# Attention scores of a head pair in one visit of TensorE, with the eighth result in the first bank, and fillers aligned to it

## The chip, the cores and the metric

One Trainium2 chip; the kernel runs on one of its cores. The metric is the device time of one execution in microseconds (us), as the median of several runs. PE is the matrix engine, DVE the vector engine, ACT the scalar engine, POOL the general one, SP the engine that issues most transfers.

## The reference, cut to what matters

One layer of an encoder on a (512, 1024) residual stream. An input projection feeds two groups that run beside each other: gated linear recurrences (forward and backward), and eight attention heads of 64 with relative bias over dilated windows. Their outputs go through `w_out`, then an MLP with squared ReLU, then a final norm.

```python
h = rms_norm(x, attn_norm_g)
xr, gate, q, k, v = split(h @ w_in)
xr = centred_depthwise_conv(xr, conv_w, conv_b)
y_rnn = (rg_lru(xr, fwd) + rg_lru(xr, bwd)) * gelu(gate)
# dilated_attention: 8 heads, patterns (window, dilation) = (128,1), (512,4), (2048,16)
logits = einsum('bqhd,bqjhd->bhqj', qb, k[:, kidx]) * 64 ** -0.5 + bias   # masked outside 0..511
out_p, lse_p = softmax(logits) @ v[:, kidx], logsumexp(logits)            # for each pattern
y_attn = sum_p softmax_p(lse_p) * out_p
x = x + concat(rms_norm(y_rnn, g1), rms_norm(y_attn, g2)) @ w_out
x = x + square(relu(rms_norm(x, g3) @ w_up)) @ w_down
return rms_norm(x, final_norm_g)
```

## The kernel before, in words

**Arithmetic.** A float32 product is made of three matmuls: both factors are split into a high part and a remainder, and `mm3` adds high x high, high x low and low x high in one PSUM bank. `conv_hi` makes the high part of a weight chunk (ACT, tile `whi`), `conv_lo` the remainder (DVE, `wlo`) and then issues the load of a later chunk (`wraw`, an SP transfer of 512 KB).

**Attention.** Positions are ordered by parity, and all three patterns are one banded score matrix with a bias table, so a query tile of 128 meets 416 keys (`NK`). The heads go in four pairs `p`; head e of a pair lies on rows 64e to 64e+63. The four query tiles of a pair have the numbers u = 0 to 3 in order of their work. `att_s` (L796 to L803 before) is the scores: for each u, three products, each for both heads, into two PSUM banks; the two heads' matmuls use 64 rows each of the array. `kks[p]` holds the keys of a pair, high and low, and behind the first 512 columns a copy of the first 256, which an SP transfer makes in `s_lo`; tiles u = 2 and 3 read into that copy. `att_e` subtracts the minimum and adds the bias on DVE (one operation for each head, PSUM to `e`) and takes the exponential on ACT. `att_t` turns three blocks of the result on PE (`pt`, banks `et`), ACT copies them to `ett`, and `att_c` turns the last 32 columns on DVE. `att_z` and `att_zd` send the reciprocal sums through DRAM and back as rows (`zd`, `zrow`), `att_av` multiplies with the values (`pav`). `load_tw` loads the bias rows of two heads (`tw`, 192 and 160 KB).

**PSUM.** Eight banks under three tags: `gs` has two, `et` two, `pj` four. A bank is taken again when its last reader is done.

**Order.** The order of every engine is that of the program text. The loop at the end of the attention part runs over i = 0 to 4 and u = 0 to 3: in round i, pair i gets its scores while pair i-1 gets its transposes. Around these stand *fillers*: one filler is one k of eight of a query or key projection (`q_thunks`, three matmuls, 0.68 us), later one of four of an output projection (`wo_thunks`). `PRE` fillers run ahead of the loop, then four in each (i, u) unless `FILL` says otherwise. `feed_q` places a weight split at two fillers of a chunk. `plan` hangs small steps (`beside`) on places (i, u, 0 to 4): among them `s_hi` and `s_lo`, which split the queries (is_k 0) and keys (is_k 1) of the next pair. SP's transfers in the loop are issued in program order too, so one that waits holds up those behind it.

Before the change a pair's scores come in two groups, u = 0 and 1, and u = 2 and 3, with eight fillers between, and a group's 12 matmuls go product by product over both tiles.

Of the kernel before, what the change touches and what calls it, by code (L numbers as in the profile page):

```python
# [28 lines left out]
NEG = -1e30  # L29
DFF = 4096  # L30
NF = DFF // P
PRE = 6
SC = (20, 21, 22, 23, 24, 25, 26, 27, 40, 41, 43, 45, 47, 49, 51, 53)
HF = NF // 2
NQ = HF // 4
# [2 lines left out]
WN = 160  # L38
# [60 lines left out]
def hybrid_kernel(ctx: ExitStack, tc, xw0, xw, xn, w_in, w_v, w_out, w_up, w_dn, gates, vecs, bias, fg, out):  # L99
# [19 lines left out]
    def ps_(name, tag):  # L119
        return psum.tile([P, S], FT, name=name, tag=tag, bufs={"pj": 4, "gs": 2, "et": 2}[tag])  # L120
# [182 lines left out]
            conv_lo(c + 3)  # L303

    def feed_q(c, k):
        if k == 1:
            conv_hi(c + 3)
        elif k == 5:
            conv_lo(c + 3)

    def mm3(o, a, b, first, last, on=False):
        nc.tensor.matmul(o, lhsT=a[0], rhs=b[0], start=bool(first), stop=False, skip_group_check=on)  # L312
# [479 lines left out]
    QT = ((1, 0), (1, 1), (0, 0), (0, 1))  # L792
    QSEQ = (0, 3, 1, 2)

    def att_s(p, us):
        for u in us:  # L796
            psq[p, u] = [ps_("ps", "pj" if u % 2 else "gs") for _ in range(2)]
        for i, (a, b) in enumerate(((0, 0), (0, 1), (1, 0))):
            for u in us:
                qt = QSEQ[u]  # L800
                w = {(0, 0): TH + TH - WN, (0, 1): 0, (1, 0): TH - WN, (1, 1): TH}[QT[qt]]
                for e, r in enumerate(halves):
                    nc.tensor.matmul(psq[p, u][e][:, :NK], lhsT=qs_[p, a][r, P * qt:P * qt + P], rhs=kks[p][r, b, w:w + NK], start=i == 0, stop=i == 2)  # L803

    def att_e(p, u):
        qt = QSEQ[u]
# [171 lines left out]
    def wo_thunks():  # L978
        order = [(0, tt, k) for tt in range(4) for k in range(4)] + [(1, tt, k) for h in (0, 2) for tt in range(4) for k in (h, h + 1)]
        pw = {}  # L980

        def end(n, tt):
            stt(x1[tt, n], pw[n, tt], rc[0][:, tt:tt + 1], x1[tt, n], op0=OP.mult, op1=OP.add)

        def mk(b, n, tt, k):
            def run():
                if k == 0:
                    pw[n, tt] = ps_("pwo", "pj")
                o = pw[n, tt]
                hi, lo = splits[C_WO + 2 * n + k // 2]  # L990
                sl, tsl = slice((k % 2) * S, (k % 2 + 1) * S), slice(tt * P, (tt + 1) * P)
                mm3(o, [t[:, tsl] for t in ycat[k]], (hi[:, sl], lo[:, sl]), k == 0, k == 3)
                if b in (1, 15, 18, 23):
                    conv_hi(C_WO + {1: 3, 15: 4, 18: 5, 23: 6}[b])
                if b in (3, 17, 20):
                    conv_lo(C_WO + {3: 3, 17: 4, 20: 5}[b])
                if n == 0 and tt and k == 1:
                    end(0, tt - 1)
                if n and (tt, k) == (0, 1):
                    end(0, 3)  # L1000
                if n and k == 3 and tt < 3:
                    end(1, tt)
            return run
        st["wo"] = lambda: end(1, 3)
        return [mk(b, *o) for b, o in enumerate(order)]
# [88 lines left out]
    def sq_(t):  # L1094
        return lambda: rnn_sq(t)
# [4 lines left out]
    def op(fn, *a):  # L1100
# [5 lines left out]
            (0, 2, 3): [add],  # L1106
            (1, 0, 2): [end(2)],
            (1, 1, 0): [sq_(2)], (1, 1, 2): [end(3)], (1, 1, 4): [add],
            (1, 3, 0): [sq_(3)], (1, 3, 2): [hi(0)], (1, 3, 3): [add, hi(1)], (2, 0, 2): [rnn_cols],
            (2, 0, 0): [lo(0), lo(1)], (2, 0, 4): [hi(2)],  # L1110
            (2, 1, 2): [hi(3)], (2, 1, 4): [lo(2)], (2, 2, 3): [lo(3)]}
    for i in range(3):
        for key, (is_k, fn) in {(0, 2): (0, s_hi), (1, 0): (0, s_lo), (2, 2): (1, s_hi), (3, 0): (1, s_lo)}.items():
            plan.setdefault((i,) + key, []).append(lambda fn=fn, a=(i + 1, is_k): fn(*a))

    def beside(*key):
# [10 lines left out]
    for key, fs in (((4, 1, 2), [(att_a, 2), (o_sum, "s1", 0), (o_sum, "s2", 0), (o_sum, "s3", 0), (o_sum, "s3", 1), (o_sum, "22", 0)]),  # L1127
# [1 line left out]
                    ((4, 3, 0), [(att_q, 2), (o_hi, "11", 1), (o_hi, "s3", 0), (o_hi, "s3", 1)]), ((4, 3, 2), [(o_lo, "11", 1), (o_lo, "s3", 0)]),  # L1129
                    ((4, 3, 4), [(att_y, 2), (o_lo, "s3", 1), (o_hi2, 0), (o_hi, "s1", 0), (o_hi, "22", 0)])):  # L1130
        plan[key] = [op(*a) for a in fs]
    FILL = {(3, 0): (1, 1, 1, 0), (3, 1): (1, 1, 1, 0), (3, 2): (1, 1, 1, 0), (4, 0): (0, 1, 0, 0), (4, 1): (0, 1, 0, 1), (4, 2): (0, 1, 0, 0), (4, 3): (0, 1, 0, 0)}


    AVS = {(2, 1): (0,), (4, 0): (1, 2)}
    with tc.manual_schedule(engines={nc.sync.engine}):
        for i in range(5):
            for u in range(4):
                if i < 4:
                    if u % 2 == 0:  # L1140
                        att_s(i, (u, u + 1))
                    if u == 2 and i < 3 or u == 0 and i:
                        for e in range(2):
                            load_tw(2 * (i + u // 2) + e, u // 2)
                if i >= 1:
                    att_t(2 * i - 2, u)
                    att_t(2 * i - 1, u)
                if i < 4:
                    att_e(i, u)
                if i >= 1:  # L1150
                    att_c(2 * i - 2, u)
                    att_c(2 * i - 1, u)
                if u == 0 and i >= 1:
                    att_z(i - 1)
                for p in AVS.get((i, u), ()):
# [7 lines left out]
                for p in AVS.get((i, u), ()):  # L1163
                    if p != 2:
                        att_y(p)
                beside(i, u, 2)
                fill(FILL.get((i, u), (1, 1, 1, 1))[2])
                beside(i, u, 3)
                fill(FILL.get((i, u), (1, 1, 1, 1))[3])
                add_x()  # L1170
                beside(i, u, 4)
    assert not plan and not more
# [631 lines left out]
```

## Time and profile before

| what | us |
|---|---|
| median of 3 runs | 526.63 (526.25 to 527.54) |
| the profiled execution | 526.41 |
| its span, first to last instruction | 524.6 |
| granted clock of TensorE | 0.999 |
| PE busy | 517.5 |
| scores (`ps`, 96 matmuls) between | 93.6 and 152.0 |

The profile's rows give a start or a count, the engine, the line, the operation and the tile written, then the tiles read. Matmuls are pipelined: one 128x512 matmul shows 0.39 us, but the next starts 0.23 us after it, so what a stretch of PE costs is read from starts, not from durations. The same holds for DVE.

### The profile page before, as it was taken

What the parts mean: (1) busy time and instruction counts of PE and PEld (TensorE: products, weight loads), DVE (VectorE), ACT (ScalarE), POOL (GpSimd) and SP (SyncE); (2) the same over time, 40 slices, a digit from 0 to 9 for tenths busy, and PEclk for the clock granted to TensorE, in tenths of its full rate; (3) what the DMA queues carried; (4) which work ended last, traced back from release to release, by engine and by line L of the source; (5) the groups of instructions that cost most, each with busy time, mean ns of one, the idle gap of its engine ahead of it and who ended that gap; (6) DMA issues with size and microseconds to landing.
All of it is one profiled execution on the core that took longest, in us unless ns stands there. A gap on an engine that the chain in (4) does not pass through costs nothing.

```text
span 524.6 us, 8198 instructions
## 1 busy us (share of the span) xinstructions
PE 517.5 (99%) x3021; PEld 443.1 (84%) x3021; DVE 430.5 (82%) x669; ACT 350.4 (67%) x566; POOL 64.0 (12%) x88
## 2 busy tenths in 40 slices
PE   9999999999999999999999999999999999999995
PEld 7867888787787688899999888889999999888884
DVE  6998986888877998898789986889656988885985
ACT  7579946668865748585578666565477677655664
POOL 0182000000000221001300312001101300140000
PEclk9999999999999999999999999999999999999999
DMA  8745545357695299847595899976978497799804
GB/s 288 237 117 166 151 152 180 107 166 208 193 292 192 78 186 279 323 128 196 136 226 144 212 272 281 314 261 161 295 224 205 111 226 219 155 285 256 196 1 161
DMA packets 39961, 104.62 MB, mean 199 GB/s; under 512 B 4944, under 2 KB 13264, under 8 KB 39920
## 3 DMA queue, kind: packets, MB, share of 16 engines
q1 hardware_dynamic: 32368, 78.10, 44.3%
q0 software_dynamic: 7408, 25.79, 26.7%
q8 instruction: 24, 0.39, 0.3%
q10 hardware_dynamic: 144, 0.20, 0.1%
q14 instruction: 17, 0.14, 0.1%
HBM read 95.59 MB, written 4.29 MB: 190 GB/s over the span
## 4 chain that ended last, share of the span: by engine, by line
PE 97%; DVE 2%; issue 0%; DVEq 0%; ACT 0%; ACTq 0%
PE pu L314 10%; PE pu L313 10%; PE pu L312 10%; PE pd L313 10%; PE pd L314 10%; PE pd L312 10%; PE pqk L312 3%; PE pqk L314 3%; PE pqk L313 3%; PE pwo L312 2%; PE pav L939 2%; PE pwo L314 2%; PE pwo L313 2%; PE pt L839 2%; PE ps L803 2%; PE pp L312 1%
## 5 line engine op out<-in xcount | busy, mean ns | idle before, releaser
L269 DVE TENSOR_TENSOR wlo<-wraw,whi 128x1024 fp32r<-128x1024 f32 x71 | 86.7, 1222 | 23.3 <-ACT whi L247 23.1
L247 ACT ACTIVATE whi<-wraw 128x1024 fp32r<-128x1024 f32 x67 | 70.7, 1057 | 33.1 <-PE pd L314 18.2
L313 PE MATMUL pd<-wlo,ah 128*128 128x512 f32 (+1 forms) x195 | 75.3, 386 | 0.0
L312 PE MATMUL pd<-whi,ah 128*128 128x512 f32 (+1 forms) x195 | 75.2, 386 | 0.0
L314 PE MATMUL pd<-whi,al 128*128 128x512 f32 (+1 forms) x195 | 75.2, 386 | 0.0
L247 ACT ACTIVATE whi<-tw 128x1024 fp32r<-128x1024 f32 x38 | 40.2, 1059 | 37.5 <-DMA tw<-in_w_up_dram 12.3
L314 PE MATMUL pu<-hh,wlo 128*128 128x256 f32 x224 | 63.4, 283 | 0.0
L313 PE MATMUL pu<-hl,whi 128*128 128x256 f32 x224 | 63.4, 283 | 0.0
L312 PE MATMUL pu<-hh,whi 128*128 128x256 f32 x224 | 63.4, 283 | 0.0
L269 DVE TENSOR_TENSOR wlo<-tw,whi 128x1024 fp32r<-128x1024 f32 x38 | 46.4, 1222 | 17.8 <-ACT whi L247 17.8
L312 PE MATMUL pu<-h2h,whi 128*128 128x256 f32 (+1 forms) x200 | 60.1, 301 | 0.0
L314 PE MATMUL pu<-h2h,wlo 128*128 128x256 f32 (+1 forms) x200 | 60.0, 300 | 0.0
L313 PE MATMUL pu<-h2l,whi 128*128 128x256 f32 (+1 forms) x200 | 60.0, 300 | 0.0
L247 ACT ACTIVATE whi<-ts 128x1024 fp32r<-128x1024 f32 x24 | 25.5, 1061 | 26.6 <-PE pd L314 17.8
L313 PEld LDWEIGHTS pu<-hl,whi 128*128 128x128 f32 x224 | 43.0, 192 | 0.0
L312 PEld LDWEIGHTS pu<-hh,whi 128*128 128x128 f32 x224 | 43.0, 192 | 0.0
L314 PEld LDWEIGHTS pu<-hh,wlo 128*128 128x128 f32 x224 | 43.0, 192 | 0.0
L312 PEld LDWEIGHTS pd<-whi,ah 128*128 128x128 f32 x195 | 36.6, 188 | 7.5
L314 PEld LDWEIGHTS pd<-whi,al 128*128 128x128 f32 x195 | 36.6, 188 | 7.3
L313 PEld LDWEIGHTS pd<-wlo,ah 128*128 128x128 f32 x195 | 36.6, 188 | 7.3
L269 DVE TENSOR_TENSOR wlo<-ts,whi 128x1024 fp32r<-128x1024 f32 x24 | 29.3, 1222 | 12.5 <-ACT whi L247 12.4
L312 PEld LDWEIGHTS pu<-h2h,whi 128*128 128x128 f32 x200 | 38.3, 191 | 1.3
(275 smaller groups left out, 1225.3 us busy)
## 6 DMA issues: line engine op xcount, KB each, us to landing
wraw<-in_w_up_dram SPq DMA_DIRECT2D x25, 512.0 KB, 4.8
ts<-in_w_dn_dram POOLq DMA_DIRECT2D x24, 512.0 KB, 12.6
wraw<-in_w_dn_dram SPq DMA_DIRECT2D x24, 512.0 KB, 8.7
tw<-in_w_up_dram SPq DMA_DIRECT2D x15, 512.0 KB, 9.2
tw<-in_w_up_dram POOLq DMA_DIRECT2D x15, 512.0 KB, 8.3
wraw<-in_w_in_dram SPq DMA_DIRECT2D x13, 512.0 KB, 4.1
ts<-in_w_dn_dram SPq DMA_DIRECT2D x8, 512.0 KB, 6.5
tw<-in_w_dn_dram SPq DMA_DIRECT2D x8, 512.0 KB, 7.6
```

The lines of the kernel that those rows point to most:

```text
L247: act(hi, raws[i], AF.Copy)
L269: nc.vector.tensor_tensor(lo, r, f(splits[i][0]), op=OP.subtract)
L312: nc.tensor.matmul(o, lhsT=a[0], rhs=b[0], start=bool(first), stop=False, skip_group_check=on)
L313: nc.tensor.matmul(o, lhsT=a[0], rhs=b[1], start=False, stop=False, skip_group_check=on)
L314: nc.tensor.matmul(o, lhsT=a[1], rhs=b[0], start=False, stop=bool(last), skip_group_check=on)
L803: nc.tensor.matmul(psq[p, u][e][:, :NK], lhsT=qs_[p, a][r, P * qt:P * qt + P], rhs=kks[p][r, b, w:w + NK], start=i == 0, stop=i == 2)
L839: nc.tensor.transpose(pt[:, i * P:(i + 1) * P], en[h][qt][:, k:k + P], ident)
L939: nc.tensor.matmul(pav[p][a, co], lhsT=vs[:, jt, h * DH:(h + 1) * DH], rhs=et[h, jt][:, ci], start=jt == 0 and i == 0, stop=jt == 3 and i ...
```

## The change

The scores of tiles 0 to 2 of a pair are issued together, tile by tile, then the DVE reads of tile 0, then the scores of tile 3, whose second head takes the `gs` bank that tile 0's first head has left. So 24 matmuls stand in a row on seven banks and one taken twice. Pair 3 keeps two groups of two tiles. The transposes that stood behind the scores at u = 0 move behind two fillers. `PRE` goes from 6 to 8, so that a projection ends just ahead of each group, and pair 3's last place loses two fillers. The weight splits of the projections move to the fourth filler of a chunk and the second of the next, the key splits from (2, 2) and (3, 0) to (2, 1) and (2, 3), and two bias loads to the end of a pair's round.

```diff
--- before.py
+++ after.py
@@ -29,7 +29,7 @@
 NEG = -1e30
 DFF = 4096
 NF = DFF // P
-PRE = 6
+PRE = 8
 SC = (20, 21, 22, 23, 24, 25, 26, 27, 40, 41, 43, 45, 47, 49, 51, 53)
 HF = NF // 2
 NQ = HF // 4
@@ -303,10 +303,10 @@
             conv_lo(c + 3)
 
     def feed_q(c, k):
-        if k == 1:
+        if k == 1 and c > C_QK:
+            conv_lo(c + 2)
+        elif k == 3:
             conv_hi(c + 3)
-        elif k == 5:
-            conv_lo(c + 3)
 
     def mm3(o, a, b, first, last, on=False):
         nc.tensor.matmul(o, lhsT=a[0], rhs=b[0], start=bool(first), stop=False, skip_group_check=on)
@@ -792,15 +792,16 @@
     QT = ((1, 0), (1, 1), (0, 0), (0, 1))
     QSEQ = (0, 3, 1, 2)
 
-    def att_s(p, us):
+    def att_s(p, us, tags):
         for u in us:
-            psq[p, u] = [ps_("ps", "pj" if u % 2 else "gs") for _ in range(2)]
-        for i, (a, b) in enumerate(((0, 0), (0, 1), (1, 0))):
-            for u in us:
-                qt = QSEQ[u]
-                w = {(0, 0): TH + TH - WN, (0, 1): 0, (1, 0): TH - WN, (1, 1): TH}[QT[qt]]
+            psq[p, u] = [ps_("ps", t) for t in tags[2 * u:2 * u + 2]]
+        for u in us:
+            qt = QSEQ[u]
+            w = {(0, 0): TH + TH - WN, (0, 1): 0, (1, 0): TH - WN, (1, 1): TH}[QT[qt]]
+            for i, (a, b) in enumerate(((0, 0), (0, 1), (1, 0))):
                 for e, r in enumerate(halves):
                     nc.tensor.matmul(psq[p, u][e][:, :NK], lhsT=qs_[p, a][r, P * qt:P * qt + P], rhs=kks[p][r, b, w:w + NK], start=i == 0, stop=i == 2)
+
 
     def att_e(p, u):
         qt = QSEQ[u]
@@ -992,8 +993,8 @@
                 mm3(o, [t[:, tsl] for t in ycat[k]], (hi[:, sl], lo[:, sl]), k == 0, k == 3)
                 if b in (1, 15, 18, 23):
                     conv_hi(C_WO + {1: 3, 15: 4, 18: 5, 23: 6}[b])
-                if b in (3, 17, 20):
-                    conv_lo(C_WO + {3: 3, 17: 4, 20: 5}[b])
+                if b in (2, 3, 17, 20):
+                    conv_lo(C_WO + {2: 2, 3: 3, 17: 4, 20: 5}[b])
                 if n == 0 and tt and k == 1:
                     end(0, tt - 1)
                 if n and (tt, k) == (0, 1):
@@ -1106,11 +1107,11 @@
             (0, 2, 3): [add],
             (1, 0, 2): [end(2)],
             (1, 1, 0): [sq_(2)], (1, 1, 2): [end(3)], (1, 1, 4): [add],
-            (1, 3, 0): [sq_(3)], (1, 3, 2): [hi(0)], (1, 3, 3): [add, hi(1)], (2, 0, 2): [rnn_cols],
+            (1, 3, 0): [sq_(3)], (1, 3, 2): [hi(0)], (1, 3, 3): [hi(1)], (2, 0, 1): [add], (2, 0, 2): [rnn_cols],
             (2, 0, 0): [lo(0), lo(1)], (2, 0, 4): [hi(2)],
-            (2, 1, 2): [hi(3)], (2, 1, 4): [lo(2)], (2, 2, 3): [lo(3)]}
+            (2, 1, 0): [hi(3)], (2, 1, 2): [lo(2)], (2, 1, 4): [lo(3)]}
     for i in range(3):
-        for key, (is_k, fn) in {(0, 2): (0, s_hi), (1, 0): (0, s_lo), (2, 2): (1, s_hi), (3, 0): (1, s_lo)}.items():
+        for key, (is_k, fn) in {(0, 2): (0, s_hi), (1, 0): (0, s_lo), (2, 1): (1, s_hi), (2, 3): (1, s_lo)}.items():
             plan.setdefault((i,) + key, []).append(lambda fn=fn, a=(i + 1, is_k): fn(*a))
 
     def beside(*key):
@@ -1129,27 +1130,37 @@
                     ((4, 3, 0), [(att_q, 2), (o_hi, "11", 1), (o_hi, "s3", 0), (o_hi, "s3", 1)]), ((4, 3, 2), [(o_lo, "11", 1), (o_lo, "s3", 0)]),
                     ((4, 3, 4), [(att_y, 2), (o_lo, "s3", 1), (o_hi2, 0), (o_hi, "s1", 0), (o_hi, "22", 0)])):
         plan[key] = [op(*a) for a in fs]
-    FILL = {(3, 0): (1, 1, 1, 0), (3, 1): (1, 1, 1, 0), (3, 2): (1, 1, 1, 0), (4, 0): (0, 1, 0, 0), (4, 1): (0, 1, 0, 1), (4, 2): (0, 1, 0, 0), (4, 3): (0, 1, 0, 0)}
+    FILL = {(3, 0): (1, 1, 1, 0), (3, 1): (1, 1, 1, 0), (3, 2): (1, 1, 1, 0), (3, 3): (0, 1, 1, 0), (4, 0): (0, 1, 0, 0), (4, 1): (0, 1, 0, 1), (4, 2): (0, 1, 0, 0), (4, 3): (0, 1, 0, 0)}
 
 
     AVS = {(2, 1): (0,), (4, 0): (1, 2)}
+    ALL, TWO = ("gs", "gs", "et", "et", "pj", "pj", "pj", "gs"), ("gs", "gs", "pj", "pj", "gs", "gs", "pj", "pj")
+
+    def att_p(i, u):
+        for fn in (att_t, att_c):
+            for h in (2 * i - 2, 2 * i - 1):
+                fn(h, u)
+
     with tc.manual_schedule(engines={nc.sync.engine}):
         for i in range(5):
             for u in range(4):
-                if i < 4:
-                    if u % 2 == 0:
-                        att_s(i, (u, u + 1))
-                    if u == 2 and i < 3 or u == 0 and i:
-                        for e in range(2):
-                            load_tw(2 * (i + u // 2) + e, u // 2)
-                if i >= 1:
-                    att_t(2 * i - 2, u)
-                    att_t(2 * i - 1, u)
-                if i < 4:
+                first = i < 3 and u == 0
+                if first:
+                    att_s(i, range(3), ALL)
+                    att_e(i, 0)
+                    att_s(i, (3,), ALL)
+                    att_e(i, 1)
+                elif i == 3 and u % 2 == 0:
+                    att_s(i, (u, u + 1), TWO)
+                if i < 3 and u == 1:
+                    for e in range(2):
+                        load_tw(2 * i + 2 + e, 1)
+                if i >= 1 and not first:
+                    att_p(i, u)
+                if i < 3 and 0 < u < 3:
+                    att_e(i, u + 1)
+                if i == 3:
                     att_e(i, u)
-                if i >= 1:
-                    att_c(2 * i - 2, u)
-                    att_c(2 * i - 1, u)
                 if u == 0 and i >= 1:
                     att_z(i - 1)
                 for p in AVS.get((i, u), ()):
@@ -1163,10 +1174,15 @@
                 for p in AVS.get((i, u), ()):
                     if p != 2:
                         att_y(p)
+                if i >= 1 and first:
+                    att_p(i, u)
                 beside(i, u, 2)
                 fill(FILL.get((i, u), (1, 1, 1, 1))[2])
                 beside(i, u, 3)
                 fill(FILL.get((i, u), (1, 1, 1, 1))[3])
+                if i < 3 and u == 3:
+                    for e in range(2):
+                        load_tw(2 * i + 2 + e, 0)
                 add_x()
                 beside(i, u, 4)
     assert not plan and not more
```

Three places show what moves. First PE, at the first score group (of pair 0 before; `ps_968` and `ps_969` are the two heads of tile 0, `ps_970` and `ps_971` of tile 1). Before:

```order
L803 MATMUL ps_968<-kk_937,qh_898 128x416
L803 MATMUL ps_969<-kk_937,qh_898 128x416
L803 MATMUL ps_970<-kk_937,qh_898 128x416
L803 MATMUL ps_971<-kk_937,qh_898 128x416
L803 MATMUL ps_968<-kk_937,ql_904 128x416
L803 MATMUL ps_969<-kk_937,ql_904 128x416
L803 MATMUL ps_970<-kk_937,ql_904 128x416
L803 MATMUL ps_971<-kk_937,ql_904 128x416
L312 MATMUL pqk_941<-h_hi_95,whi_837 128x512
```

(The product high x low stands between the two shown and reads like the first.) In the change, pair 1's group, from tile 1's last product to the group's end; `ps_1136` is tile 2's first head, `ps_1165` and `ps_1166` are tile 3's two heads, and in brackets stands the semaphore that a row waits for (DMAHW7 that of the copy of the keys, DVE that of DVE's reads; rows that only repeat are left out):

```order
L803 MATMUL ps_1134<-kk_1092,ql_1062 128x416
L803 MATMUL ps_1135<-kk_1092,ql_1062 128x416
L803 MATMUL ps_1136<-kk_1092,qh_1036 128x416 [waits DMAHW7_49]
L803 MATMUL ps_1137<-kk_1092,qh_1036 128x416
L803 MATMUL ps_1136<-kk_1092,ql_1062 128x416
L803 MATMUL ps_1137<-kk_1092,ql_1062 128x416
L803 MATMUL ps_1165<-kk_1092,qh_1036 128x416
L803 MATMUL ps_1166<-kk_1092,qh_1036 128x416 [waits DVE_49]
L803 MATMUL ps_1165<-kk_1092,ql_1062 128x416
L803 MATMUL ps_1166<-kk_1092,ql_1062 128x416
```

Tile 2, with its need of the copy, stands right behind tile 1 now, and the 20th matmul waits for a read of the same group.

Second DVE, at the key split of pair 1 during pair 0's round (`kraw` the projection, `kk` the remainder, `e` a read of scores). Before:

```order
L762 TENSOR_TENSOR kraw_1082<-pqk_1007,rrow_337 128x512
L612 TENSOR_TENSOR ysq_1003<-ysq_1003,ysq_1031 128x512
L819 ISA e_1096,mn_1097<-ps_1048,tw_639 128x416
L819 ISA e_1100,mn_1101<-ps_1049,tw_642 128x416
L781 TENSOR_TENSOR kk_1084<-kraw_1082,kk_1084 128x512
L269 TENSOR_TENSOR wlo_1118<-wraw_927,whi_1094 128x1024
L819 ISA e_1157,mn_1158<-ps_1122,tw_1062 128x416
```

In the change:

```order
L762 TENSOR_TENSOR kraw_1078<-pqk_1023,rrow_337 128x512
L820 ISA e_1080,mn_1081<-ps_1005,tw_639 128x416
L820 ISA e_1084,mn_1085<-ps_1006,tw_642 128x416
L269 TENSOR_TENSOR wlo_1097<-wraw_908,whi_1046 128x1024
L612 TENSOR_TENSOR ysq_1034<-ysq_1034,ysq_1067 128x512
L781 TENSOR_TENSOR kk_1092<-kraw_1078,kk_1092 128x512
L758 SCALAR_TENSOR_TENSOR qraw_1124<-pqk_1088,rrow_337 128x512
L820 ISA e_1157,mn_1158<-ps_1132,tw_1048 128x416
```

(Rows of `mn` alone, which belong to the reads, are left out.) The remainder of the keys now stands behind a weight split, and the next query projection ahead of the next pair's first read.

Third SP, at the copy of pair 2's keys. Before:

```order
L876 DMA zrow<-zd 64x1x512 [waits DMAHW5_49,DMAHW3_49]
L876 DMA zrow<-zd 64x1x512 [waits DMAHW4_49]
L782 DMA kk<-kk 128x2x256 [waits DVE_49,PE_49]
L230 DMA wraw<-in_w_out_dram 128x1024 [waits DMAHW6_49,DVE_49,Activation_49]
L476 DMA tw<-nbd 128x384 [waits DMAHW7_49]
```

In the change:

```order
L230 DMA wraw<-in_w_out_dram 128x1024 [waits DMAHW2_49,DVE_49,Activation_49]
L877 DMA zrow<-zd 64x1x512 [waits DMAHW4_49,DMAHW3_49]
L877 DMA zrow<-zd 64x1x512
L782 DMA kk<-kk 128x2x256 [waits DMAHW5_49,DVE_49,PE_49]
L476 DMA tw<-nbd 128x384 [waits DMAHW6_49]
```

The weight load, which waits for a DVE split, stands ahead of the two row loads and the copy.

## The prediction, made before the changed kernel had run

> **What bounds the kernel now.** I read four views in this order: the page's engine rows and its chain, the waits of PE, the timeline of PE around the first score groups, and then the timelines of DVE and SP at the same place.
>
> ```profile
> span 524.6 us, 8198 instructions
> PE 517.5 (99%) x3021; PEld 443.1 (84%) x3021; DVE 430.5 (82%) x669; ACT 350.4 (67%) x566; POOL 64.0 (12%) x88
> PE 97%; DVE 2%; issue 0%; DVEq 0%; ACT 0%; ACTq 0%
> PE pwarm L142 <- PEq L1793: 0.8, 1, 0.8
> ```
>
> PE is busy for 99% of the span, the chain that ended last is PE for 97%, and the whole list of PE's waits is the one row of 0.8 us at the start. So whatever PE saves or waits anywhere between its first and its last matmul moves the end by as much; DVE and ACT matter only where PE would have to wait for them. A busy row hides the price of changing from one kind of matmul to another, so I read the starts in the timeline (columns: start, duration, both in us):
>
> ```profile
> 86.06 0.39 PE L312 MATMUL pqk<-h_hi,whi 128*128 128x512 f32 x1
> ...
> 93.31 0.39 PE L314 MATMUL pqk<-h_hi,wlo 128*128 128x512 f32 x1
> 93.63 1.02 PE L803 MATMUL ps<-kk,qh 64*128 64x416 f32 x8
> 94.49 0.54 PE L803 MATMUL ps<-kk,ql 64*128 64x416 f32 x4
> 94.96 0.50 PE L312 MATMUL pqk<-h_hi,whi 128*128 128x512 f32 x1
> 95.29 0.40 PE L313 MATMUL pqk<-h_lo,whi 128*128 128x512 f32 x1
> ...
> 107.35 0.39 PE L314 MATMUL pqk<-h_hi,wlo 128*128 128x512 f32 x1
> ...
> 109.00 0.87 PE L839 MATMUL pt<-ident,e 128*128 128x128 f32 x6
> 109.63 0.48 PE L312 MATMUL pqk<-h_hi,whi 128*128 128x512 f32 x1
> ...
> 112.22 0.40 PE L314 MATMUL pqk<-h_hi,wlo 128*128 128x512 f32 x1
> ...
> 113.03 0.48 PE L312 MATMUL pqk<-h_hi,whi 128*128 128x512 f32 x1
> 113.34 0.40 PE L313 MATMUL pqk<-h_lo,whi 128*128 128x512 f32 x1
> ```
>
> From 86.06 to 93.31 lie 32 full-size matmuls: (93.31 - 86.06) / 32 = 0.2266 us from start to start, 0.000443 us a column. Twelve score matmuls of 416 columns, two at a time on the two halves of the rows, would stream in 6 x 416 x 0.000443 = 1.105 us. They take more: from 93.31 to 95.29 are 1.98 us, less two ordinary pitches (0.453) 1.53 us, so one visit to the 64-row form costs **0.42 us** beyond its streaming. Where transposes follow the scores the exit is cheaper: 107.35 to 109.63 is 2.28, less one pitch (0.227), less the 0.58 that six transposes take alone (112.22 to 113.03, less a pitch), less 1.105: **0.37 us**.
>
> **The change, part by part.** *Fewer visits.* Pair 0 goes from two visits to one: 0.42 saved. In pairs 1 and 2 two visits with the cheap exit (0.73) become one that ends in an ordinary matmul (0.42): 0.31 each. Pair 3 keeps its two groups of twelve. Sum **-1.04 us**. The number of matmuls and transposes is the same, so nothing else on PE gets shorter. The order of the three products inside a tile, and pass by tile instead of tile by pass, costs nothing that the rows show: accumulating three times running into one bank is what the 0.2266 us rows do already.
>
> *The eighth bank.* The 20th matmul writes the bank that the first DVE read of the group frees. DVE first turns the query projection that ends as the group starts, then reads the first tile, which is complete after six matmuls.
>
> ```profile
> 94.87 0.59 DVE L819 CUSTOM_DVE_ANT_0 e<-ps,tw 128x416 f32<-128x416 f32 x1 [1.64 <-PE ps L803]
> 95.39 0.58 DVE L819 CUSTOM_DVE_ANT_0 e<-ps,tw 128x416 f32<-128x416 f32 x1
> 95.90 0.69 DVE L594 TENSOR_TENSOR ga<-ga,hs 128x512 f32<-128x512 f32 x1
> 96.62 0.69 DVE L595 TENSOR_TENSOR gt<-gt,ga 128x512 f32<-128x512 f32 x1
> 97.23 0.68 DVE L758 SCALAR_TENSOR_TENSOR qraw<-pqk,rrow 128x512 f32<-128x512 f32 x1
> ...
> 100.18 0.69 DVE L785 TENSOR_TENSOR ql<-qraw,qh 128x512 fp32r<-128x512 f32 x1
> 100.78 1.22 DVE L269 TENSOR_TENSOR wlo<-wraw,whi 128x1024 fp32r<-128x1024 f32 x1
> 101.92 0.58 DVE L819 CUSTOM_DVE_ANT_0 e<-ps,tw 128x416 f32<-128x416 f32 x1
> ...
> 103.67 0.69 DVE L762 TENSOR_TENSOR kraw<-pqk,rrow 128x512 f32<-128x512 f32 x1 [0.66 <-PE pqk L314]
> 104.28 0.68 DVE L612 TENSOR_TENSOR ysq<-ysq 128x512 f32<-128x512 f32 x1
> 104.88 0.58 DVE L819 CUSTOM_DVE_ANT_0 e<-ps,tw 128x416 f32<-128x416 f32 x1
> ...
> 105.90 0.69 DVE L781 TENSOR_TENSOR kk<-kraw,kk 128x512 fp32r<-128x512 f32 x1
> ```
>
> Count from the group's first matmul. The first tile ends at about 0.11 + 2 x 0.184 + 0.35 = 0.83, DVE starts on it at 0.87 and frees the bank at 1.45 (0.58 a read). PE reaches the 20th matmul after nine pairs, 0.11 + 9 x 0.184 = 1.77. So it costs **0**, with 0.3 us to spare; it starts to cost when DVE comes to the group 0.3 us late.
>
> *The copy of the keys, the term that I look at hardest.* Tile 2 reads the part of kk that an SP transfer copies behind the first 512 columns. Before, tile 2 stood seven us behind tile 0 (93.63 and 100.64 for pair 0); now it stands six pairs behind it, 0.11 + 6 x 0.184 = 1.21 us. The step that makes the key remainders, and the copy with it, was moved forward by two fillers, and stands on DVE behind four reads of one group, and on SP behind a weight load (pairs 1 and 2) and two row loads (pair 2). Rows for the transfers (KB each, median us from issue to landing; the two hs rows are of two windows, 58 to 65 us and 73 to 75 us):
>
> ```profile
> kk<-kk SPq DMA_DIRECT2D x4, 256.0 KB, 2.6
> zrow<-zd SPq DMA_DIRECT2D x8, 128.0 KB, 4.9
> wraw<-in_w_out_dram SPq DMA_DIRECT2D x5, 512.0 KB, 3.5
> hs<-ga SPq DMA_DIRECT2D x4, 128.0 KB, 2.3
> hs<-ga SPq DMA_DIRECT2D x2, 128.0 KB, 3.2
> 73.17 0.33 SPq L230 DMA_DIRECT2D wraw<-in_w_in_dram  x1
> 74.30 1.11 SPq L515 DMA_DIRECT2D hs<-ga  x2
> 119.99 1.32 SPq L876 DMA_DIRECT2D zrow<-zd  x2
> ```
>
> Pair 1, counted from the start T of pair 0's group, DVE by pitches of the rows above: first read at 0.87, four reads 4 x 0.51, ga gt, wlo, ga gt 2 x 1.33 + 1.14, two reads 1.02, ql 0.60, kraw 0.61 (PE has it ready at 8.1, DVE comes at 8.3), two reads 1.02, wlo 1.14, ysq 0.60, kk 0.69: 12.4 us (ACT makes the high part of the keys meanwhile). The copy is issued there, a weight load 1.2 us ahead of it. PE: the group takes 1.33 + 1.105 = 2.43, sixteen fillers 48 x 0.2266 = 10.88, exit and entry 0.2, so pair 1 starts at T + 13.5 and needs the copy at 14.7. Landing after its own 2.6: 15.0, a wait of 0.3. An hs copy issued 1.1 us behind such a load landed 0.9 later than one alone (3.2 against 2.3); so much on top makes 1.2. Bounds 0.3 and 1.2; I take **0.5**, nearer the copy's own row, because the load (3.5 from its issue at T + 11.2) has landed at 14.7.
>
> Pair 2, from pair 1's start: PE delivers the keys' projection at 2.43 + 0.5 + 24 x 0.2266 + two groups of transposes at 0.67 (0.58 and 0.09 at the next start, 113.03 to 113.34) + 0.3 = 10.0. DVE then has kraw 0.61, ysq 0.60, two 32-column transposes 0.2, two reads 1.02, wlo 1.14: 13.6. SP issues the load (0.33) and the two row loads (1.32) ahead of the copy: 15.25, by when DVE has the key remainders too. PE needs it at 2.43 + 0.5 + 10.88 + 4 x 0.67 + 0.2 + 1.21 = 17.9. With its own 2.6 the copy lands at 17.85: no wait. If it lands behind the row loads, issued by 14.6 and 4.9 long, that is 19.5 or a little later: 1.6 to 1.9. Bounds 0 and 1.9; I take **1.0**. Pair 3 needs no copy before its second group, nine us in.
>
> The Trainium skill ("DMA: Bandwidth & Descriptors", section "Queues, rings and completion order") says that descriptors of one issuing queue are consumed in ring order on each DMA engine, which speaks against this change; the trace agrees as far as hs goes (2.3 alone, 3.2 behind a load). The same page's fit, 2.0 us plus the bytes at 436 GB/s (section "Anatomy of one DMA"), would have the 1.0 MB from pair 2's load through its copy land 4.4 us after 13.6, at 18.0, which is a wait of 0.1 and a sum near -0.4; the row of zrow, 4.9 us for 128 KB, does not agree with that fit, and the row decides.
>
> *The rest at no cost.* The weight splits moved by a few fillers (conv_hi at the fourth product, conv_lo at the second of the next) are used two chunks, over 10 us, later; a DVE split is 1.14 us. The bias rows loaded at the end of a pair are read by DVE 6 us into the next one, after landings of 4.9 us. The two fillers taken from the end of pair 3 stand before the loop now.
>
> **Sum.** -1.04 + 0 + 0.5 + 1.0 = **+0.5 us**. The profiled execution took 526.41 us (1.8 around its span of 524.6); the runs shown have their median 0.2 above it, at 526.63. I say 526.41 + 0.5 = **526.9 us**, no change that can be told: about 0.3%, 1.6 us, is what a measurement of this kernel can tell.
>
> **Rivals.**
>
> 1. *The copies are in time.* For it: their own row of 2.6 leaves 0.3 and 0. Against it: SP's order. Then -1.04 + 0.3 or less: 525.4 to 525.7, still within 0.3%.
> 2. *Slower: the copies take as long as the row loads.* Place: the 13th matmul of pairs 1 and 2. With 4.9 us instead of 2.6, pair 1 waits 12.4 + 4.9 - 14.7 = 2.6, and pair 2, whose chain moves with PE, 2.2: -1.04 + 4.8 = +3.8, 530.2 us. It decides from 2.6 us of waits in all. For it: zrow's 4.9 in the same queue; against it: kk's own row and the hs rows, at most 0.9 more.
> 3. *Slower: DVE comes late to the groups.* DVE is 82% busy. If it still has a split (1.22) in hand when each of the three groups starts, the eighth bank makes PE wait 1.22 - 0.3 three times, 2.7 us, on top of the sum: 529.6. Against it: in the walk DVE stands idle for the projection before each group. It decides from 0.7 us of lateness a group.
> 4. *The change does not do what it says.* If the 0.42 belong to each tile's first product and not to the change of form, nothing is saved: +1.5, 527.9. Against it: the extra lies at 93.31 to 93.63 and 94.96 to 95.29, at both ends.
> 5. *Faster by more than 0.3%.* PE has two more gaps behind the attention, where it waits for DVE's results:
>
> ```profile
> 180.29 0.39 PE L314 MATMUL pwo<-whi,ol 128*128 128x512 f32 x1
> 180.76 0.50 PE L312 MATMUL pwo<-whi,oh 128*128 128x512 f32 x1
> ...
> 182.01 0.40 PE L314 MATMUL pwo<-whi,ol 128*128 128x512 f32 x1
> 182.48 0.50 PE L312 MATMUL pwo<-whi,oh 128*128 128x512 f32 x1
> ```
>
> Each loses 0.47 - 0.23 and 0.1 at the next start. If the shifted splits free DVE there, 0.7 us go too: with copies in time 524.6 to 525.0. Against it: that DVE chain starts from a PE result and moves with it.
>
> **How the numbers follow.** The forecast 0.40, rival 1 0.15, rival 4 0.05: within 0.3% together 0.60. Rival 2 0.18 and rival 3 0.12: slower 0.30, kept that high since DVE's lateness and SP's queue only add. Rival 5 0.10. The range runs from 525.2, rival 1 with a little of rival 5, to 529.2, which takes in both upper bounds of the copies (-1.04 + 1.2 + 1.9 = +2.1, 528.5) and the smaller half of rivals 2 and 3; about 0.07 lies below and 0.13 above.
>
> **What would show it.** Right: five score visits instead of eight, each first full-size matmul after them still some 0.1 late; PE's waits list a transfer kk<-kk (or an idle stretch at the 13th score matmul) for pairs 1 and 2, with 1 to 2 us in all; no gap before the 20th. Rival 1 shows no gap in the groups, rival 2 gaps above 2 us, rival 3 gaps at the 20th released by DVE, rival 5 a shorter stretch at 180 to 183. Wrong would be a time outside 525 to 528.5 with no gap in the groups: then something behind them moved that I hold to be unchanged.

## The result, and the profile after

| what | before | after |
|---|---|---|
| median, us | 526.90 (526.25 to 527.54, 4 runs) | 532.71 (532.50 to 533.45, 4 runs) |
| ratio to before | 1 | 1.0112, 95% interval 1.0101 to 1.0124 |
| the profiled execution, us | 526.41 | 532.58 |
| its span, us | 524.6 | 529.8 |

The change makes the kernel 5.8 us slower. The forecast was 526.9, at most 529.2. The first rows of the page after, and the whole list of PE's waits (us in total, times, longest us):

```profile
span 529.8 us, 8188 instructions
PE 518.2 (98%) x3021; PEld 443.3 (84%) x3021; DVE 430.7 (81%) x669; ACT 350.2 (66%) x566; POOL 63.9 (12%) x88
```

```profile
PE pwo L312 <- DVE mn L820: 1.9, 1, 1.9
PE ps L803 <- DMA kk<-kk: 1.7, 2, 0.9
PE pwarm L142 <- PEq L1809: 0.8, 1, 0.8
PE pwo L312 <- DVE x L984: 0.7, 1, 0.7
PE pt L840 <- ACT e L821: 0.3, 1, 0.3
```

Before, the list had the row of pwarm alone. There are two families of new waits: on the copy of the keys, which the prediction had, and three rows from pair 3's round, which it did not have: two of the output projection (`pwo`) and one of the transposes (`pt`). To weigh them apart I cut the attention in two by PE's starts: the first score matmul, pair 3's first score matmul, and the first matmul of the last values group. Before (timeline of PE; the first score matmul, 93.63, stands in the prediction):

```profile
143.99 0.83 PE L803 MATMUL ps<-kk,qh 64*128 64x416 f32 x6
...
171.31 0.92 PE L939 MATMUL pav<-ett,vs 128*64 128x416 f32 x4
```

After:

```profile
95.14 0.64 PE L803 MATMUL ps<-kk,qh 64*128 64x416 f32 x4
...
146.71 0.64 PE L803 MATMUL ps<-kk,qh 64*128 64x416 f32 x4
...
176.56 3.02 PE L940 MATMUL pav<-ett,vs 128*64 128x416 f32 x24
```

Pairs 0 to 2 take 50.36 us before (143.99 - 93.63) and 51.57 after: **+1.21**. Pair 3 takes 27.32 before (171.31 - 143.99) and 29.85 after, but after it holds two fillers less, six matmuls at 0.2266, 1.36 us: **+3.89** for the same work. Together +5.10, of the 5.2 by which the span grew. So three quarters of the loss lie in the pair whose scores the change leaves alone.

*Pairs 0 to 2.* The timeline of PE at the groups of pairs 1 and 2 (start, duration, in brackets the idle time and what ended it):

```profile
109.37 0.54 PE L803 MATMUL ps<-kk,qh 64*128 64x416 f32 x4
109.75 0.35 PE L803 MATMUL ps<-kk,ql 64*128 64x416 f32 x2
110.84 0.64 PE L803 MATMUL ps<-kk,qh 64*128 64x416 f32 x4 [0.74 <-DMA kk<-kk]
...
127.08 0.35 PE L803 MATMUL ps<-kk,ql 64*128 64x416 f32 x2
128.37 0.65 PE L803 MATMUL ps<-kk,qh 64*128 64x416 f32 x4 [0.94 <-DMA kk<-kk]
```

The step that should be one pitch of 0.184 is 1.09 and 1.29: 0.90 and 1.11 lost, both at the 13th matmul, none at the 20th, where the group takes its first bank again.

*Pair 3.* DVE and SP in the changed kernel (the SP rows are issues; x2 are two loads in a row, of which the first is the block `x(2,0)`):

```profile
152.08 0.08 DVE L820 DVE_READ_ACCUMULATOR2_ANT mn<- 128x1 f32 x1
157.13 0.75 DVE L984 SCALAR_TENSOR_TENSOR x<-pwo,rcol,x 128x512 f32<-128x512 f32 x1 [4.96 <-DMA x<-in_xn_dram]
157.79 1.21 DVE L1057 TENSOR_TENSOR tw<-ws 128x1024 f32<-128x1024 f32 x1
```

```profile
144.71 0.64 SPq L782 DMA_DIRECT2D kk<-kk  x1
145.39 0.61 SPq L1047 DMA_DIRECT2D x<-in_xn_dram  x1
...
148.00 0.47 SPq L1050 DMA_DIRECT2D ws<-in_w_out_dram  x1
149.22 0.59 SPq L872 DMA_DIRECT2D zd<-zt  x1
149.86 2.36 SPq L1047 DMA_DIRECT2D x<-in_xn_dram  x2
```

DVE adds each finished output block to its residual block, and stands 4.96 us for `x(2,0)`. Everything behind it in DVE's order stands too, among it the reads of pair 3's third score tile. Before, the same two places:

```profile
153.43 0.71 DVE L983 SCALAR_TENSOR_TENSOR x<-pwo,rcol,x 128x512 f32<-128x512 f32 x1
```

```profile
147.71 0.95 SPq L1046 DMA_DIRECT2D x<-in_xn_dram  x2
```

and the first of these two loads in the list of transfers (count, KB, us from issue to landing):

```profile
x<-in_xn_dram SPq DMA_DIRECT2D x1, 256.0 KB, 4.3
```

Counted from pair 3's first score, the load is issued 3.72 us in before (147.71) and 3.15 in after, so a little earlier; but DVE comes for it 9.44 us in before and 5.45 after (152.16, the end of the row at 152.08). Two fillers earlier is here not 1.36 us but four, because the place moves over the end of a round, with its transposes and the second score group. And the load is slower, some 7 us (149.86 to 157.13) instead of 4.3. So the 4.96 us have two parts: DVE comes 4.0 us earlier, of which 1.4 were in hand and 0.6 are made up by the earlier issue, which leaves 2.0; the other 3.0 are the slower load. PE's losses behind it, in its timeline:

```profile
156.86 0.40 PE L314 MATMUL pwo<-whi,yl 128*128 128x512 f32 x1
157.93 0.50 PE L312 MATMUL pwo<-whi,yh 128*128 128x512 f32 x1 [0.68 <-DVE x L984]
...
159.84 0.40 PE L314 MATMUL pwo<-whi,yl 128*128 128x512 f32 x1
162.10 0.50 PE L312 MATMUL pwo<-whi,yh 128*128 128x512 f32 x1 [1.86 <-DVE mn L820]
...
163.47 1.07 PE L840 MATMUL pt<-ident,e 128*128 128x128 f32 x5 [0.30 <-ACT e L821]
```

1.07 and 2.26 from start to start instead of 0.2266, so 0.84 and 2.03; then 0.8 at pair 3's transposes (the 40 steps between them sum to 5.28 us, before to 4.47), which wait because ACT's exponentials are as late as DVE's reads. That is 3.7 of the 3.89.

### The profile page after: what moved, and what is told of

The parts are those of the page before. It is cut to its first block, busy times and chain, and to the rows that moved or that the text cites. A ratio compares the mean times of both kernels' runs of the same rounds, so it can differ in the third digit from the quotient of the medians.

```text
span 529.8 us, 8188 instructions
## 1 busy us (share of the span) xinstructions
PE 518.2 (98%) x3021; PEld 443.3 (84%) x3021; DVE 430.7 (81%) x669; ACT 350.2 (66%) x566; POOL 63.9 (12%) x88
## 4 chain that ended last, share of the span: by engine, by line
PE 89%; DVE 5%; DMA 2%; ACT 1%; SPq 1%; issue 1%; DVEq 0%; ACTq 0%
PE pu L312 10%; PE pu L314 10%; PE pu L313 10%; PE pd L314 10%; PE pd L313 10%; PE pd L312 10%; PE pav L940 2%; PE pwo L312 2%; PE pqk L312 2%; PE pqk L314 2%; PE pqk L313 2%; PE pwo L314 2%; PE pwo L313 2%; PE pp L312 1%; PE pp L313 1%; PE pp L314 1%
## 5 line engine op out<-in xcount | busy, mean ns | idle before, releaser
L313 PEld LDWEIGHTS pu<-h2l,whi 128*128 128x128 f32 x200 | 38.3, 191 | 1.3
L314 PEld LDWEIGHTS pu<-h2h,wlo 128*128 128x128 f32 x200 | 38.3, 191 | 1.3
```

The lines of the kernel that those rows point to most:

```text
L313: nc.tensor.matmul(o, lhsT=a[0], rhs=b[1], start=False, stop=False, skip_group_check=on)
L314: nc.tensor.matmul(o, lhsT=a[1], rhs=b[0], start=False, stop=bool(last), skip_group_check=on)
```

## The experiments

Twelve kernels ran, each against the kernel before on the same chip. The table gives for each the two stretches as cut above, against before, in its profiled execution (with 1.36 us added to the stretch that holds two fillers less), and the medians of all runs.

| run | pairs 0 to 2 | pair 3 | median, us | ratio to before, 95% interval |
|---|---|---|---|---|
| the change | +1.21 | +3.89 | 532.71 | 1.0112 (1.0101 to 1.0124) |
| e1_x_early | +1.36 | +3.81 | 531.01 | 1.0078 (1.0056 to 1.0099) |
| e2_tw_back | +1.40 | +1.93 | 530.58 | 1.0074 (1.0054 to 1.0094) |
| e3_x_early_kk_act | +8.19 | +0.50 | 535.61 | 1.0153 (1.0129 to 1.0177) |
| e4_before_align | 0.00 | +5.57 | 532.46 | 1.0092 (1.0066 to 1.0117) |
| e5_fill | +1.42 | +2.79 | 531.45 | 1.0086 (1.0073 to 1.0099) |
| e6_fill_tw | +1.10 | +0.02 | 528.15 | 1.0025 (1.0016 to 1.0035) |
| e7_fill_tw_kk | -1.03 | +0.66 | 526.62 | 0.9997 (0.9988 to 1.0006) |
| e8_fill_tw_kk_two | +0.05 | +0.49 | 527.79 | 1.0018 (1.0009 to 1.0026) |
| e9_fill_tw_kk2 | -1.04 | +0.63 | 525.98 | 0.9984 (0.9975 to 0.9992) |
| e10_kk_only | -1.02 | +3.51 | 530.76 | 1.0076 (1.0062 to 1.0090) |
| e11_before_align_early | -0.02 | +1.25 | 528.85 | 1.0036 (1.0023 to 1.0049) |
| e12_loads_first | +1.08 | +0.49 | 529.21 | 1.0043 (1.0031 to 1.0056) |

What the table leaves out: ahead of the first score the profiled executions differ by up to 1.5 us beyond the two fillers (e12; 0.6 in e9), behind the last values group by up to 0.7 (e4, e8), and the runs of one kernel by up to 3.0 (e3). So the stretches and the medians need not add up to better than that.

### The late block loaded earlier (e1)

```diff
-        more.append([x_in(1, 0)])
+        more.append([x_in(1, 0), x_in(2, 0)])
...
-        more.append([sum1, x_in(2, 0), x_in(3, 0), w_in(b21, "21")])
+        more.append([sum1, x_in(3, 0), w_in(b21, "21")])
```

> Only the load of the third residual block x(2,0) is issued three places earlier, together with x(1,0). Theory (DVE stands 4.96 us on that load in the changed kernel, and PE loses 0.85 + 2.03 + 0.46 + 0.24 us of starts behind it): DVE's wait on x goes, 3.0 to 3.8 us come back, 529 to 529.7 us; the two waits on the copy of the keys (0.9 and 1.1) stay. Rival (DVE has too much work there, the load only coincides): the reads of the scores stay late, 531.5 us or more.

Measured 531.01, between the two forecasts: 1.7 better than the change and at least 1.3 worse than the theory had it. The timeline of DVE shows why:

```profile
152.43 0.75 DVE L984 SCALAR_TENSOR_TENSOR x<-pwo,rcol,x 128x512 f32<-128x512 f32 x1 [0.22 <-PE pwo L314]
156.88 1.23 DVE L1057 TENSOR_TENSOR tw<-ws 128x1024 f32<-128x1024 f32 x1 [3.70 <-DMA ws<-in_w_out_dram]
```

`x(2,0)` is in time, and DVE stands 3.70 us at the very next operation that reads a load, the weight block `ws`, which stands behind four bias-row loads. The wait is not that of one load; it is that of the whole order of loads.

### The bias rows of pair 3 put back (e2)

```diff
+                if i == 3 and u == 0:
+                    for e in range(2):
+                        load_tw(2 * i + e, 0)
...
-                if i < 3 and u == 3:
+                if i < 2 and u == 3:
```

> Only pair 3's second two bias loads go back to the start of its round, behind the 512 KB weight load instead of ahead of it. Theory (the residual block is wanted two fillers earlier, the bytes ahead of it in SP's queue are the same): at most 0.5 us better, 532.2 to 532.7. Rival (the swapped order of the loads made the block late): x(2,0) lands as soon as before, 3 us come back, about 529.5 us.

Measured 530.58, between the two forecasts; pair 3 falls from +3.89 to +1.93, and DVE still stands 3.00 us ahead of the sum with `x(2,0)`. So half of pair 3's loss goes with these four loads behind the weight block again, a move that the prediction held to be free.

### The copy of the keys issued by ACT (e3)

```diff
-            nc.sync.dma_start(f(k[:, :, S:]), f(k[:, :, :TH]))
+            nc.scalar.dma_start(f(k[:, :, S:]), f(k[:, :, :TH]))
```

(on top of e1)

> As e1_x_early, and the copy of the keys is issued from ACT's queue instead of SP's. Theory (in pair 2 the copy is late because it is issued behind a weight load and two row loads on SP, in pair 1 because DVE makes the remainder late): pair 2's wait of 1.1 us falls under 0.3, pair 1's of 0.9 to 0.3 to 0.9, so 0.8 to 1.5 us better than e1_x_early. Rival (the copy is late because DVE is late in both): both waits stay, the same time as e1_x_early.

Measured 535.61, 4.6 worse than e1, which neither forecast had. PE in its timeline, and pair 2's copy in the list of transfers (count, KB, us from issue to landing):

```profile
114.58 0.64 PE L803 MATMUL ps<-kk,qh 64*128 64x416 f32 x4 [3.45 <-DMA kk<-kk]
...
116.67 0.63 PE L313 MATMUL pqk<-h_lo,whi 128*128 128x512 f32 x1
117.10 0.63 PE L314 MATMUL pqk<-h_hi,wlo 128*128 128x512 f32 x1
```

```profile
kk<-kk ACTq DMA_DIRECT2D x1, 256.0 KB, 5.5
```

In the changed kernel, on SP (two copies):

```profile
kk<-kk SPq DMA_DIRECT2D x2, 256.0 KB, 3.5
```

The copy takes 5.5 us instead of 3.5. Pair 1's is issued 1.2 us behind the weight load as in the change (108.58 and 107.37, there 107.54 and 106.34), but PE goes on 6.0 us after its issue instead of 3.3. In the change the bias-row loads that follow in program order are issued behind the copy (from 108.21 on); here SP issues them from 107.75 on, and they run ahead of the copy and beside it. In the long wait PE also lost its clock (below). So SP's order harms the copy by what is ahead of it and shields it from what is behind. That the copy loses its time to those loads is likely, but no run held them back on SP to show it.

### The alignment alone (e4), and with its two fillers taken elsewhere (e11)

The kernel before, in e4 with this edit, in e11 with `(2, 3)` in place of `(3, 3)` in the last line, which goes into `FILL`:

```diff
-PRE = 6
+PRE = 8
...
+        (3, 3): (0, 1, 1, 0),
```

> The kernel before with eight fillers ahead of the loop instead of six and two less at the end of pair 3, and nothing else. Theory (the alignment brings the use of x(2,0) two fillers forward and its load not): DVE waits 1 to 3 us on x(2,0), whose load was 1.5 us early before; 0.3 to 2 us slower than before, 527.2 to 529. Rival (the alignment is free, the lateness comes from the loads that the change moved): within 0.3 us of before.

Measured 532.46: without any new grouping, without moved splits or bias rows, the two shifted fillers alone cost about as much as the whole change. That is beyond both forecasts; even its two shortest runs (531.03 and 531.30) are above 529. DVE's row and PE's waits are like those of the change, and below them stands the issue of the load:

```profile
157.15 0.75 DVE L983 SCALAR_TENSOR_TENSOR x<-pwo,rcol,x 128x512 f32<-128x512 f32 x1 [4.87 <-DMA x<-in_xn_dram]
```

```profile
PE pwo L312 <- DVE mn L819: 1.7, 1, 1.7
PE pwo L312 <- DVE x L983: 1.2, 1, 1.2
```

```profile
149.98 0.94 SPq L1046 DMA_DIRECT2D x<-in_xn_dram  x2
```

The load of `x(2,0)` takes 7.1 us here (149.98 to landing), as slow as in the change, although e4 leaves the bias rows where they were. The expectation counted only the earlier use, which by the starts is worth 2.0 of the 4.87 us, and not the slower load.

> The kernel before with two more fillers ahead of the loop, as in e4_before_align, but the two left out in round (2,3) instead of (3,3). Theory A (not the alignment costs the time, but that the output-projection fillers come before their loads): as before the change, 526.6 to 527.3. Rival B (the aligned projections cost it): 530 or more, as e4_before_align's 532.46.

Measured 528.85, below rival B and 1.6 above the upper end of theory A. Pairs 0 to 2 are at -0.02, so the aligned projections cost nothing, as A has it; pair 3 keeps +1.25. The two fillers now missing ahead of pair 3's scores had covered DVE's key remainder, which the kernel before makes only in that last place, (2, 3): PE waits for it directly, which the expectation overlooked. By the starts 0.81 of the 1.25 lie between score matmuls, 0.61 of them in the step of the row below, 0.28 between transposes and 0.16 between fillers.

```profile
145.89 0.65 PE L803 MATMUL ps<-kk,qh 64*128 64x416 f32 x4 [0.33 <-DVE kk L781]
```

### The two fillers taken ahead of pair 3 in the change (e5, e6)

```diff
-        (3, 3): (0, 1, 1, 0),
+        (2, 3): (0, 1, 1, 0),
```

e6 has the edit of e2 as well.

> The changed kernel with the two fillers left out at the end of pair 2's third-indexed round (2,3) instead of (3,3), so that from pair 3 on the output-projection fillers stand against their loads as before the change, while the projections stay aligned to the loop. Theory A (the fillers came two earlier than their loads, DVE stands in order behind x(2,0), PE loses some 4 us): no DVE wait on x(2,0), and if the weight load that still stands behind four bias-row loads is in time, 528.0 to 529.0; if that load is now the late one, up to 530.5, with DVE waiting on ws. Rival B (the moved weight splits or the group of four tiles make DVE and PE lose the time): 532 to 533 as the changed kernel.

Measured 531.45, 0.95 above the worse case named. The wait for `x(2,0)` is gone, and the weight block behind the bias rows is the late one, by 4.91 us:

```profile
151.84 0.75 DVE L984 SCALAR_TENSOR_TENSOR x<-pwo,rcol,x 128x512 f32<-128x512 f32 x1
157.49 1.22 DVE L1057 TENSOR_TENSOR tw<-ws 128x1024 f32<-128x1024 f32 x1 [4.91 <-DMA ws<-in_w_out_dram]
```

> As e5_fill, and the bias rows of pair 3's last two tiles loaded at the start of pair 3 again, behind the weight load, as before the change. Theory A: the late loads are gone altogether, only the copies of the keys are left: 527.0 + 2.0 - 1.0 = 528.0, between 527.5 and 528.6, and PE's waits list nothing but kk and the start. Rival B: 531.5 or more.

Measured 528.15, as expected: pair 3 is back at +0.02, and of PE's waits only the copies are left. So pair 3's loss is these two things together and nothing else: fillers that come before their loads, and bias rows put ahead of a weight block. The two do not simply add: with the bias rows alone put back +1.93 stay (e2), with the fillers alone +2.79 (e5).

### The loads put first instead (e12)

The edits of e1 and e2 together, fillers as in the change.

> The changed kernel with its fillers as they are, but x(2,0) and the next weight load issued ahead of the four bias-row loads (e1_x_early and e2_tw_back together). Theory A (either the fillers later or the loads earlier mends it): 532.7 - 3.8 = 528.9, at best 528.2; if the load of the second weight block is now the late one, 530. Rival B: 530.5 or more, as with each of the two alone.

Measured 529.21, pair 3 at +0.49. The loads in the order of their use mend pair 3 nearly as well as e6's later fillers do.

### The key splits forward (e7, e9, e10)

```diff
-(2, 1): (1, s_hi), (2, 3): (1, s_lo)}
+(2, -1): (1, s_hi), (2, 0): (1, s_lo)}
...
+                beside(i, u, -1)
                 if i < 3 and 0 < u < 3:
                     att_e(i, u + 1)
```

e7 has this and e6's edits; e9 leaves pair 3's splits, i = 2, at (2, 1) and (2, 3); e10 is the change with e9's splits alone.

> As e6_fill_tw, and the two steps that split the next pair's keys moved forward in the third round (the high part ahead of the reads of the fourth score tile, the remainder and the copy ahead of the fillers, so ahead of a weight split on DVE and of a weight load and two row loads on SP). Copy issued 1.5 to 2.4 us earlier than at 107.54 and 124.80. Theory A: no wait at the 13th score matmul of any pair: 526.0, between 525.5 and 526.6, faster than before the change by the 1.04 of the visits. Rival C (the copy is slow because of what the DMA engines carry, not where it stands): 0.5 to 1.5 us of the wait stay, 526.8 to 527.8.

Measured 526.62, pairs 0 to 2 at -1.03: the copies' waits are gone, and rival C with them. The 0.6 above the forecast are in pair 3, where SP now stood at pair 3's copy ahead of the first residual block.

> As e7_fill_tw_kk, but the key steps of pair 3, whose copy is not needed early, stay where the change has them, so that SP does not stand at that copy ahead of the first residual block. e7_fill_tw_kk showed DVE waiting 2.68 us for x until 146.28 and PE losing 0.59 behind it. Theory A: that gap goes, 526.62 - 0.6 = 526.0, between 525.6 and 526.3, faster than before the change by 0.8 us (0.15%). Rival: the gap moves to the next load, 526.4 to 526.8.

Measured 525.98. The copies and pair 1's group in it:

```profile
kk<-kk SPq DMA_DIRECT2D x2, 256.0 KB, 2.5
```

```profile
110.17 0.35 PE L803 MATMUL ps<-kk,ql 64*128 64x416 f32 x2
110.36 0.54 PE L803 MATMUL ps<-kk,qh 64*128 64x416 f32 x4
```

The 13th matmul follows one pitch (0.19) behind the 12th. By the medians this kernel is faster than both, if only just: 0.9984 of before (0.9975 to 0.9992), 1.0 us, and 6.7 us better than the change. That it met its forecast is in part luck. The profiled execution, one of the longer ones (526.74), is no shorter than before (span 524.7 against 524.6): to the -1.04 of pairs 0 to 2 come +0.63 in pair 3 and 0.6 ahead of the attention. In pair 3 e7's wait for `x` is gone, as theory A says, but DVE now waits for a bias row, as its rival says, and PE's starts lose some 0.6 after it; that the one causes the other is not shown (e6 has such a wait of 1.48 and loses nothing in pair 3):

```profile
154.41 0.59 DVE L820 CUSTOM_DVE_ANT_0 e<-ps,tw 128x416 f32<-128x416 f32 x1 [1.64 <-DMA tw<-nbd]
```

> The changed kernel with the key steps of pairs 1 and 2 moved forward alone; fillers and loads of pair 3 as the change has them. Theory A (the waits on the copies and those on the late loads add, since the loads are issued as the kernel goes on): 532.7 - 2.0 = 530.7, between 530.2 and 531.3, x(2,0) still waited for. Rival (they overlap: what PE gains at the copies it waits longer for the loads): 532 to 533.

Measured 530.76, as the sum said: the waits on the copies and on the loads add.

### Two groups again in the mended kernel (e8)

```diff
-                first = i < 3 and u == 0
+                first = False
...
-                elif i == 3 and u % 2 == 0:
+                elif i < 4 and u % 2 == 0:
...
-                if i < 3 and 0 < u < 3:
-                    att_e(i, u + 1)
-                if i == 3:
+                if i < 4:
                     att_e(i, u)
```

> As e7_fill_tw_kk, with the scores of pairs 0 to 2 in two groups of two tiles again (eight visits instead of five). Theory A with the price of a visit from the starts of PE (0.42, 0.31, 0.31): 1.0 us slower than e7_fill_tw_kk, 526.5 to 527.5, no different from before the change. Rival D (the visits cost nothing of themselves): the same as e7_fill_tw_kk within 0.3.

Measured 527.79, 1.2 above e7 and 0.3 above the range that its expectation gave: the kernel is not back at the time before, but 0.18% slower (0.09 to 0.26%). Pairs 0 to 2 stand at +0.05 with eight visits and at -1.03 with five: three visits less, with the transposes at u = 0 behind two fillers, are worth 1.08 in the same kernel, where the prediction had 1.04. Rival D falls.

## Why the prediction was wrong, step by step

- **Visits, -1.04: right.** e9 against before gives -1.04 over pairs 0 to 2, e7 against e8 -1.08. Rival 4 (nothing saved) falls.
- **Eighth bank, 0: right.** No gap at any 20th matmul; rival 3 falls.
- **Copies, +1.5: the mechanism right, the size short.** Pair 1 waited 0.90 (0.5 taken, 0.3 to 1.2 given), pair 2 1.11 (1.0 taken, 0 to 1.9 given): 2.01, and some 0.2 more as PE takes up work behind each (the stretch is +1.21, and -1.04 + 2.01 is +0.97). The term that was short is the transfer, taken at 2.6 us: the copies were issued 2.4 and 2.5 us before the 13th matmul could start (107.54 and 124.80, against 109.93 and 127.26), and landed 3.3 and 3.6 us after their issue. The order on SP was the cause: ahead of the loads the copy takes 2.5 us, behind them 3.5, and the wait is gone in e7 and e9. The Trainium skill ("DMA: Bandwidth & Descriptors", section "Queues, rings and completion order") says that descriptors of one issuing queue are consumed in ring order on each DMA engine, and the 2.5 and 3.5 agree with that. The fit in that page's section "Anatomy of one DMA", which the page gives for transfers issued on the gpsimd path and not for SP's, would have pair 2 wait 0.1; 1.11 was measured. Rival 2, waits above 2.6 in all, did not come. Pair 3's second group stands 6.6 us into its round (143.99 to 150.60 before) and not nine, which changes nothing: no copy was waited for there.
- **The rest at no cost: this step failed.** The moved weight splits were free (pairs 0 to 2 are at +0.05 in e8). But "the two fillers taken from the end of pair 3 stand before the loop now" cost some 3.9 us with the bias rows, e4 shows as much for the fillers alone (3.9 and 4.2 above before in its two shortest runs), and e6 takes it away. The step named no work that hides the shift, and it did not ask what each shifted filler reads. Its last instruction is DVE's sum with a residual block from a load of the same round; in the trace before, that load took 4.3 us from 147.71 and DVE came at 153.43, so 1.4 us were in hand, and the shift was four. That accounts for 2.0 of DVE's 4.96 us; the other 3.0 are the load itself, 7.3 us instead of 4.3, which the step did not consider either. "The bias rows loaded at the end of a pair are read by DVE 6 us into the next one" looked at the rows' own landing and not at the weight block that they push back on the same queue.
- **Rivals.** None of the five named this wait. Rival 5's gaps at 180 to 183 stayed as they were: from start to start the change has 0.47 and 0.46 at 185.54 and 187.27, and e9 0.46 and 0.46.
- **The form of the sum.** +0.5 became -1.04 + 2.01 + 0.2 + 3.9 = +5.1 in the profiled execution, whose span grew by 5.2. Its time grew by 6.2; the 1.0 outside the span no run explains.

What stays open: why `x(2,0)` needs some 7 us after the change (149.86 to 157.13) and 4.3 before. The moved bias rows are not needed for it: e4 and e11, which leave them, have 7.1 and 6.9. The loads of pair 3 stand closer together on SP there (4.0 us from the copy of its keys to `x(2,0)`, 146.00 to 149.98 in e4, against 5.2 before, 142.50 to 147.71); in the change it is 5.2 too, but with `x(1,0)` among them. No run held the spacing alone.

## What to carry to other kernels

A shift of "two fillers" is no shift by two fillers' time: write down for every piece of work that moves what it reads, when that was loaded, and how much slack the trace shows, and count the round ends that it moves over. On an engine that works in order a late load costs whatever stands behind it, so mending one load moves the wait to the next; mend the order of the loads as a whole, by first use. When a change bundles a gain with an alignment, run the alignment alone: here one kernel (e4) would have told that the scores were not the matter.

## What the runs showed of the hardware

PE's granted clock fell after waits of about two us, and not each time. In e3 (columns: window, length, busy time and count of PE, PEld, DVE, ACT, POOL, then granted clock, DMA share, GB/s), behind the waits of 3.45 and 2.09 us:

```profile
116.00:120.00 4.00, 4.00 (x16) 3.20 (x15) 1.07 (x5) 0.54 (x2) 0.00 (x0) 0.62 0.96 281
136.00:140.00 4.00, 4.00 (x17) 3.21 (x14) 3.83 (x11) 0.27 (x1) 0.00 (x0) 0.57 0.32 89
```

128x512 matmuls start 0.43 us apart in the first of these stretches (116.67 to 117.10) instead of 0.2266. e1, behind a wait of 1.85 us, and the changed kernel, behind one of 1.86, at the same place:

```profile
160.00:164.00 4.00, 2.80 (x11) 1.73 (x13) 4.00 (x10) 4.00 (x11) 0.00 (x0) 0.70 0.73 230
```

```profile
160.00:164.00 4.00, 1.84 (x9) 0.93 (x7) 4.00 (x11) 4.00 (x12) 0.00 (x0) 1.00 0.53 175
```

So the profiled execution of e1 shows pair 3 no better than the change (+3.81) although its wait is one less: what it saved, it lost to the clock, which was at 0.50 in each us from 162 to 165. In e5 and e10 it stayed at 1.00 behind waits of 1.8 and 1.9. e4's +5.57 holds such a dip too, in which runs of the same kernel differ (531.03 at a mean clock of 0.997, 533.63 at 0.994). So in these runs a stall of PE of this length cost its own time alone or some two us more. The Trainium skill ("TensorE: Matmul & The Clock Gate", section "What's actually happening") states that the clock falls to half after at least one idle window of about 3.4 us, and that this window runs freely. The half agrees with e1's 0.50; the length does not, since here waits of some two us were enough, and no run shows where a window begins.
